# Later landing times in a planner, other homes for one branch's operands, and one branch product as four pairs of seven block products

## The chip, the cores and the metric

The kernel runs on one core of one Trainium2 chip. The metric is the device time of one execution in microseconds (us), the median of several runs, on the same chip for the kernels that are compared. TensorE multiplies matrices and writes to PSUM banks; VectorE and ScalarE do elementwise work and read the banks; GpSimd does some more; SyncE issues most of the transfers. Each engine works through its own queue in order.

## The reference

One layer of a decoder on 512 tokens of 1,024 channels, in fp32. A normed input is projected to everything that three branches need; each branch's output is gated and multiplied by its own square matrix, the three are summed under further gates, and a last product and a norm follow.

```python
h = rmsnorm(x, norm_g)
(aq, ak, av, ao, az, ai, af, bq, bk, bv, bz, bf, cu, cz, gates) = jnp.split(h @ w_in, SPLIT_POINTS, axis=-1)
hA = mlstm_chunkwise(conv and silu of aq, ak; av; ai, af)      # 4 heads of 256
yA = norm(hA) * ml_norm_g * sigmoid(ao) * silu(az)
yB = forgetting_attention(bq, bk, bv, bf) * silu(bz)           # 8 heads of 128
yC = multiscale_pool(cu, pool_w, pool_scale) * silu(cz)
yb = einsum('bsnw,nwd->bsnd', stack([yA, yB, yC], axis=2), w_branch)   # 3 x (512x1024 by 1024x1024)
merged = sum(sigmoid(gates) * yb, axis=2)
out = rmsnorm(x + merged @ w_out, final_g)
```

## The kernel before, in words

**Arithmetic.** Every fp32 operand is split into a high part (a cast to the type that TensorE multiplies, on ScalarE, `hi_of`, L288) and a low part (the rest, a subtraction on VectorE, `lo_of`, L291). A product is three matmuls, high by high, high by low and low by high (`mm3`, L300 to L302). Activations lie transposed, channels on the partitions and the 512 tokens along the row.

**Units and pairs.** A `unit` makes 128 output channels: 8 steps over the 1,024 input channels, 24 matmuls of 512 columns in one bank. A `pair` makes 256 output channels by a Strassen-Winograd scheme: the 2 by 2 block product takes seven block products (12 matmuls of 256 columns each, 84 in all) where two units take 48 matmuls of 512 columns. For it the activations come as seven operands (the blocks `A11`, `A12`, `A22` and the sums `s1` to `s4`, made once for all pairs of the same activations), and the weights as blocks and their sums, made for each pair. The weights of a pair come by two loads on SyncE's queue (L376, L380) and one that adds in flight on GpSimd's; VectorE adds two more sums (L294). A pair uses three of the four banks that projections have, named `x`, `yz` and `y4`; each holds more than one block product in turn, so between them ScalarE copies what is there into a side tile `e`. TensorE may not write the next block product into the bank before that copy is done:

```python
side(yz[:, H:], e[:, 2])                                    # ScalarE, L494
prod(x_[:, :H], 2, 0, sig["s2"], False, True, last=True)    # into x, on top
side(x_[:, :H], e[:, 1], -1.0)                              # ScalarE, L496
```

The block products of one pair follow each other in the banks `x`, `yz`, `yz`, `x`, `y4`, `yz`, `x`. In the trace a bank is named by what it makes and the pair's first number: `ak_ak_5x` is bank `x` of the pair that makes head 2's `ak`.

**What sets the order.** Nothing is ordered by hand. While the program is built, a planner (`Flow`) keeps a clock for each engine and a list of generators. Each of these says with `yield (engine, cost, earliest)` that its next instruction runs on that engine, for how long, and not before when; the planner always writes the instruction that can start first by its clocks. Tiles and banks are counted resources (`"w"` for 512-column work tiles, `"C"` and `"E"` for 1,024-column tiles, `"pj"` for the banks). So a number such as the `2.5` after a load, the time at which the load is taken to have landed, sets where the instruction that reads it stands in its engine's queue. Weights are prepared up to five items of TensorE's order ahead.

**The order of the work.** First the norm and head 0 of the mLSTM; heads 1 to 3 (`aq`, `ak`, `az`, `ao` as pairs, one plain gate unit each); four pool groups; eight attention heads in four rounds; the last gate pairs, `g_1_4` and `g_1_6`; then the branch products in the order mLSTM (`n = 0`), pool (`n = 2`), attention (`n = 1`), each as 8 units; then the output product. The results of the branches and the sigmoids of the gates go to DRAM (`y`, `g`) as they are made and come back later: `reload` loads a branch's output in eight pieces `yf` (L1625) and splits each into a home tile, and `load_gate` loads a gate tile `gt` (L1698). The evacuation of a unit multiplies the bank by the gate (L1716, L1718) and adds it to `merged`.

For each mLSTM head, `emat` loads a row `nmb` from DRAM and makes exponentials from it on ScalarE, four times the first of these two:

```python
nc.sync.dma_start(out=nmb, in_=rows[h:h + 1, :].partition_broadcast(P))       # L925
t = yield ("POOL", 0.9, t + 2.5)
nc.scalar.activation(out=es[:, P:], in_=nmb[:, s0 + P:], func=AF.Exp, bias=ac)  # L939
nc.scalar.activation(out=es[:, :P], in_=nmm[:, s0:s0 + P], func=AF.Exp, bias=ac)  # L941
```

The operands of the first branch have two homes of the kind `b` (1,024 columns), and the other two lie in tiles that the last attention head uses until then (`pmh`, `pml`, `vhi`, `emat`). The operands of the middle branch lie in the tiles of the normed input (`hT0`, `hT1`), free once the last gate product has read them.

## Time and profile before

| | |
|---|---|
| median of 3 runs | 863.16 us (862.78 to 864.06) |
| the profiled execution | 864.43 us, span 862.6 us |
| TensorE | 840.7 us busy, 97% of the span, 5882 matmuls in the record |
| VectorE | 638.9 us, 74% |
| ScalarE | 519.8 us, 60% |
| GpSimd | 110.2 us, 13% |
| mean granted clock of TensorE | 0.992 of full speed |
| transfers | 155.80 MB, 181 GB/s on average |

The span is the time from the first to the last instruction of the profiled execution; the time of that execution has some more around it, and the median is that of other executions. Busy shares are averages over stages that differ; where an engine waits is shown by the views of waits, of the chain of work and of the timeline.

### The profile page before, as it was taken

The numbers are of one execution on the slowest core, as the hardware profiler recorded it, in microseconds if no ns is written. First come the engines' busy times: TensorE is split into PE (matmuls) and PEld (weight loads), VectorE is DVE, ScalarE is ACT, GpSimd is POOL, SyncE is SP. The second block draws the span as 40 slices with busy tenths as digits, with TensorE's granted clock in tenths as the row PEclk, the third lists the DMA queues.
The fourth block names the chain that finished last, engine by engine and source line by source line (L and its number), as shares of the span: only waits on it lengthen the run. The fifth ranks groups of instructions, "written<-read, shape, count | busy, mean of one in ns | idle before, by whom it ended". The sixth has DMA issues, their size and how long they took to land.

```text
span 862.6 us, 14921 instructions
## 1 busy us (share of the span) xinstructions
PE 840.7 (97%) x5882; PEld 790.1 (92%) x5882; DVE 638.9 (74%) x1015; ACT 519.8 (60%) x881; POOL 110.2 (13%) x141
## 2 busy tenths in 40 slices
PE   8999999997999999999999999999999899999997
PEld 7888899997999999999999999999999778888886
DVE  4888987786988858888888787878877663445622
ACT  7569788747959748445567686567668532112323
POOL 0001521001110001011221222121210000000020
PEclk9999999998999999999999999999999999999999
DMA  9327865483684558487766876487873875564302
GB/s 342 104 75 224 223 163 155 140 255 89 171 244 102 149 152 234 148 219 204 195 209 172 248 198 177 112 250 199 233 180 116 305 267 192 171 244 132 106 32 98
DMA packets 60230, 155.80 MB, mean 181 GB/s; under 512 B 5364, under 2 KB 8820, under 8 KB 60160
## 3 DMA queue, kind: packets, MB, share of 16 engines
q1 hardware_dynamic: 45600, 125.91, 41.7%
q0 software_dynamic: 13840, 27.82, 19.9%
q10 hardware_dynamic: 720, 1.13, 0.4%
q8 instruction: 46, 0.75, 0.3%
q14 instruction: 24, 0.20, 0.1%
HBM read 140.13 MB, written 14.70 MB: 179 GB/s over the span
## 4 chain that ended last, share of the span: by engine, by line
PE 77%; DMA 10%; ACT 6%; DVE 5%; issue 1%; SPq 1%; POOL 0%; DVEq 0%; ACTq 0%; POOLq 0%
PE wb L302 4%; DMA R_None<-w_pairs 4%; PE wb L300 4%; PE wb L301 4%; DMA nmb<-rows 2%; PE out L302 2%; PE out L300 2%; PE out L301 2%; DVE lo L291 1%; DMA yf<-y 1%; ACT hi L288 1%; PE av L301 1%; PE av L302 1%; PE av L300 1%; DMA x<-x_in 1%
## 5 line engine op out<-in xcount | busy, mean ns | idle before, releaser
L291 DVE TENSOR_TENSOR lo<-R_None,hi 128x1024 fp32r<-128x1024 f32 (+1 forms) x168 | 180.8, 1087 | 31.7 <-ACT hi L288 31.0
L288 ACT CAST hi<-R_None 128x1024 fp32r<-128x1024 f32 (+1 forms) x168 | 153.6, 944 | 30.4 <-DVE R_None L294 17.2
L288 ACT CAST hi<-raw 128x1024 fp32r<-128x1024 f32 (+3 forms) x53 | 52.6, 1003 | 67.3 <-DMA raw<-w_units 59.4
L383 POOL DMA_DIRECT2D R_None<-w_pairs x42 | 51.1, 1217 | 328.4 <-DMA R_None<-w_pairs 172.3
L291 DVE TENSOR_TENSOR lo<-raw,hi 128x1024 fp32r<-128x1024 f32 (+3 forms) x53 | 61.1, 1161 | 14.4 <-ACT hi L288 14.1
L294 DVE TENSOR_TENSOR R_None<-R_None 128x512 f32<-128x512 f32 x84 | 58.1, 692 | 5.0 <-DMA R_None<-w_pairs 4.2
L1718 DVE TENSOR_TENSOR gt<-wb,gt 128x512 f32<-128x512 f32 x16 | 11.1, 691 | 37.2 <-PE wb L302 37.2
L1499 POOL TENSOR_SCALAR_AFFINE_SELECT nfb<-nfb 128x128 f32<-128x128 f32 x32 | 20.3, 643 | 73.9 <-DMA nfb<-rows 65.2
L291 DVE TENSOR_TENSOR lo<-R,hi 128x1024 fp32r<-128x1024 f32 (+1 forms) x24 | 25.7, 1083 | 3.3 <-ACT hi L288 3.3
L288 ACT CAST m<-mg 128x512 fp32r<-128x512 f32 x8 | 5.0, 621 | 35.8 <-DVE mg L294 35.8
L301 PE MATMUL out<-lo,m 128*128 128x512 f32 (+1 forms) x72 | 26.3, 366 | 0.0
L300 PE MATMUL out<-hi,m 128*128 128x512 f32 (+1 forms) x72 | 26.3, 366 | 0.0
L302 PE MATMUL out<-hi,m 128*128 128x512 f32 (+1 forms) x72 | 26.3, 366 | 0.0
L288 ACT CAST hi<-R 128x1024 fp32r<-128x1024 f32 (+1 forms) x24 | 21.9, 941 | 5.0 <-DVE R L294 3.2
L302 PE MATMUL wb<-yc,lo 128*128 128x512 f32 x64 | 24.9, 389 | 0.0
L300 PE MATMUL wb<-yc,hi 128*128 128x512 f32 x64 | 24.9, 389 | 0.0
L301 PE MATMUL wb<-yc,hi 128*128 128x512 f32 x64 | 24.9, 389 | 0.0
L1753 DVE TENSOR_TENSOR res<-out,res 128x512 f32<-128x512 f32 (+1 forms) x9 | 5.7, 632 | 17.9 <-PE out L302 17.8
L1756 ACT ACTIVATE fsq<-res 128x512 f32<-128x512 f32 (+1 forms) x9 | 5.3, 584 | 22.6 <-DVE res L1753 22.6
L1536 ACT ACTIVATE s<-s,mn 128x128 f32<-128x128 f32 (+3 forms) x32 | 17.7, 555 | 1.8 <-DVE mn L1525 1.7
L1525 DVE CUSTOM_DVE_ANT_0 s<-sB,nfb 128x128 f32<-128x128 f32 (+3 forms) x32 | 14.3, 486 | 5.4 <-issue 5.2
L960 DVE SCALAR_TENSOR_TENSOR cvaq<-aq,cs,cvaq 128x511 f32<-128x511 f32 (+2 forms) x18 | 13.4, 742 | 6.0 <-ACT cvaq L957 6.0
(2320 smaller groups left out, 3424.1 us busy)
## 6 DMA issues: line engine op xcount, KB each, us to landing
R_None<-w_pairs SPq DMA_DIRECT2D x42, 768.0 KB, 7.1
raw<-w_units SPq DMA_DIRECT2D x46, 512.0 KB, 4.3
R_None<-w_pairs SPq DMA_DIRECT2D x42, 512.0 KB, 5.2
R_None<-w_pairs POOLq DMA_DIRECT2D x42, 512.0 KB, 6.8
g<-g SPq DMA_DIRECT2D x12, 512.0 KB, 4.5
yf<-y SPq DMA_DIRECT2D x24, 256.0 KB, 5.6
gt<-g SPq DMA_DIRECT2D x24, 256.0 KB, 4.2
R<-w_pairs SPq DMA_DIRECT2D x6, 768.0 KB, 6.5
```

What stands on the lines that cost most here:

```text
L288: nc.scalar.copy(out=hi, in_=full)
L291: nc.vector.tensor_tensor(out=lo, in0=full, in1=hi.bitcast(F32), op=ALU.subtract)
L294: nc.vector.tensor_tensor(out=out_, in0=a, in1=c, op=ALU.add)
L300: nc.tensor.matmul(out_, lhsT=ah, rhs=bh, start=start, stop=False, **kw)
L301: nc.tensor.matmul(out_, lhsT=ah, rhs=bl, start=False, stop=False, **kw)
L302: nc.tensor.matmul(out_, lhsT=al, rhs=bh, start=False, stop=stop, **kw)
L383: nc.gpsimd.dma_start(out=r[:, 3 * Q:].rearrange("p (a c) -> p a c", a=2), in_=src[:, 3 * Q:].unsqueeze(1).to_broadcast([P, 2, Q]), accum_ ...
L960: nc.vector.scalar_tensor_tensor(out=acc[:, j:], in0=srcs[c][:, :S - j], scalar=col(C_CONV, ci * 4 + 3 - j), in1=acc[:, j:], op0=ALU.mult, ...
L1499: nc.gpsimd.affine_select(out=nf[i][:, i * P:], in_=nf[i][:, i * P:], pattern=[[-1, P]], compare_op=ALU.is_ge, fill=NEG, base=0, channel_m ...
L1525: nc.vector.tensor_tensor_reduce(out=ss[i][:, :n], in0=os_[i][:, :n], in1=nf[i], scale=-P ** -0.5, scalar=-NEG, op0=ALU.add, op1=ALU.min, ...
L1536: nc.scalar.activation(out=s_, in_=s_, func=AF.Exp, bias=ms[i][0], scale=-1.0, accum_out=sme)
L1718: nc.vector.tensor_tensor(out=g_, in0=o, in1=g_, op=ALU.mult)
```

## The change

1. **Landing times.** The planner's times from the issue of a load to its reader go up: `rows` 2.5 to 4.5, `nmb` 2.5 to 6.8, `nfb` (attention) 4.0 to 8.0, `yf` 2.5 to 6.0, `gt` 2.5 to 4.6, and those of the stores of `y` and `g`.
2. **Homes.** The operands of the first branch go to `b` tiles, all but one low part; the second half of `merged` goes to the tiles that held them. Loads of `yf` may be issued as soon as the first home is free; the reload of the third branch is queued after the first branch's units.
3. **The middle branch.** Its product is made by four pairs. A new function, `sides_c`, makes the seven operands from eight loads `ycf`; a pair's result is merged by two multiplies of 512 columns and one sum of 1,024.

```diff
@@ -82,7 +82,10 @@
     for n in (0, 2, 1):
-        u += [("U", "wb", n, d) for d in range(KT)]
+        if n == 2:
+            u += [("P", ("wb", n, 2 * i), ("wb", n, 2 * i + 1)) for i in range(KT // 2)]
+        else:
+            u += [("U", "wb", n, d) for d in range(KT)]
...
@@ -923,7 +926,7 @@
             nc.sync.dma_start(out=nmb, in_=rows[h:h + 1, :].partition_broadcast(P))
-            t = yield ("POOL", 0.9, t + 2.5)
+            t = yield ("POOL", 0.9, t + 6.8)
...
@@ -1618,12 +1621,13 @@
                 ty = yield ("wait", ("y", n, i))
-                th = yield ("wait", ("home", n, i))
+                yield ("wait", ("home", n, 0))
                 tw = yield ("get", "w", 1)
                 t = yield ("SP", 0.06, max(tw, ty))
                 f_ = work(f"yf{n}{i}{c}")
                 nc.sync.dma_start(out=f_, in_=yd[n, i][:, c])
-                t = yield ("ACT", a_cost(S), max(t + 2.5, th))
+                th = yield ("wait", ("home", n, i))
+                t = yield ("ACT", a_cost(S), max(t + 6.0, th))
...
@@ -1639,34 +1643,85 @@
-            return (tg("pmh"), tg("pml")) if i == 2 else (tg("vhi"), tg("emat"))
+        def home(nm):
+            def at(i):
+                if i == 3:
+                    lo = st.tile([P, 2, S], F32R, tag="emat", name=f"{nm}3l", bufs=1)
+                    return b(f"{nm}3h", (P, 2, S), F32R), lo
+                return [b(f"{nm}{i}{x_}", (P, 2, S), F32R) for x_ in ("h", "l")]
+            return at
...
+        def sides_c():
+
+            big = [st.tile([P, 4, 4, H], F32R, tag=f"hT{i}", name=f"yc{i}", bufs=1) for i in range(2)]
+            t = yield ("get", "E", 2)
+            f_ = [b(f"ycf{q}", (P, 4, H)) for q in range(4)]
+            tq = []
+            for q in (2, 3, 0, 1):
+                for i in range(2):
+                    ty = yield ("wait", ("y", 2, 2 * (q % 2) + i))
+                    t = yield ("SP", 0.06, max(t, ty))
+                    nc.sync.dma_start(out=f_[q][:, 2 * i:2 * i + 2],
+                                      in_=yd[2, 2 * (q % 2) + i][:, :, (q // 2) * H:(q // 2 + 1) * H])
+                tq.append(t + 9.0)
+            done = {}
+
+            def parts(name, q, home, t):
+                t = yield ("ACT", a_cost(D), t)
+                hi, lo = home if home else [b(f"yc{name}{x_}", (P, 4, H), F32R) for x_ in ("h", "l")]
+                hi_of(hi, f_[q])
+                t = yield ("DVE", v_cost(D), t)
+                lo_of(lo, f_[q], hi)
+                sig_c[name] = (hi, lo)
+                done[name] = t
+
+            def total(o, a_, c_, op, t):
+                t = yield ("DVE", v_cost(D), t)
+                nc.vector.tensor_tensor(out=f_[o], in0=f_[a_], in1=f_[c_], op=op)
+                done["f", o] = t
...
+            t = max(tq)
+            yield from parts("A22", 3, home(0), t)
+            yield from parts("A11", 0, home(1), t)
+            yield from total(3, 2, 3, ALU.subtract, done["A22"])
+            yield from parts("A12", 1, home(2), t)
+            yield from total(2, 0, 2, ALU.subtract, done["f", 3])
+            yield from parts("s1", 3, home(3), done["f", 3])
+            yield from total(0, 3, 0, ALU.subtract, done["f", 3])
+            yield from total(1, 1, 0, ALU.add, max(done["f", 0], done["A12"]))
+            yield from parts("s2", 0, None, done["f", 0])
+            yield from parts("s4", 1, None, done["f", 1])
+            yield from parts("s3", 2, None, done["f", 2])
...
@@ -1680,11 +1735,10 @@
         fl.add(free_a(), 1)
-        reload(0, home_a, 1)
+        reload(0, home("ya"), 1)
         while gates_left:
             filler()
-        fl.put("w", 2)
-        homes_left()
+        fl.add(sides_c(), 1)
...
@@ -1696,7 +1750,7 @@
                 nc.sync.dma_start(out=g_, in_=gd[n, d // 2][:, d % 2])
-                fl.done["gt", n, d] = t + 2.5
+                fl.done["gt", n, d] = t + 4.6
...
         branch(0, True, False)
-        for name, k in (("qk", 2), ("v", 1)):
-            fl.put(name, k)
-        branch(2, False, False)
+        for i in range(4):
+            fl.done["home", 1, i] = fl.t["PE"]
+        reload(1, home("yb"), 2)
+        fl.need(("ys", 2))
+        for i in range(KT // 2):
+            cell = [None]
+
+            def merge(cell, i, t):
+                c_ = cell[0]
+                for c in range(2):
+                    tg = yield ("wait", ("gt", 2, 2 * i + c))
+                    t = yield ("DVE", v_cost(S), max(t, tg))
+                    nc.vector.tensor_tensor(out=c_[:, c], in0=c_[:, c], in1=gate.pop((2, 2 * i + c)),
+                                            op=ALU.mult)
+                    fl.put("w", 1, t)
+                t = yield ("DVE", v_cost(D), t)
+                add(merged[i], merged[i], c_)
+                fl.put("C", 1, t)
+
+            for c in range(2):
+                load_gate(2, 2 * i + c)
+            pair(("wb", 2, 2 * i), ("wb", 2, 2 * i + 1), two(cell, f"ybc{i}"),
+                 lambda t, cell=cell, i=i: fl.add(merge(cell, i, t), 1), sig_c)
```

Over the whole program TensorE has 5994 instructions instead of 5850, VectorE 1044 instead of 1017, ScalarE 852 instead of 827, GpSimd 150 instead of 146, SyncE as many as before. Below stand instructions as they follow each other in an engine's queue, before the change and after it; the lines of the changed kernel have other numbers (L288 is L291, L494 and L496 are L497 and L499, L939 is L942).

**The third head.** ScalarE's queue before the change, at head 2's `ak` pair (`ak_4_ak_5`: its bank copies are those of `x`, `yz`, `x`, `y4`):

```order
L494 COPY ak_4_ak_5e_2085<-ak_4_ak_5yz_2087 128x256
L288 CAST pAl1_2023<-e1_1424 128x128
L957 ACTIVATE cvaq21_2146<-aq2_2047,cs_71 128x512
L939 ACT_TABLE_LOAD
L939 ACTIVATE e2_2143<-nmb2_2137,aT_203 128x384
L496 ACTIVATE ak_4_ak_5e_2085<-ak_4_ak_5x_2068 128x256
L494 COPY ak_4_ak_5e_2085<-ak_4_ak_5y4_2150 128x256
L941 ACTIVATE e2_2143<-nmm2_2139,aT_203 128x128
```

After the change, at the same pair:

```order
L497 COPY ak_4_ak_5e_2088<-ak_4_ak_5yz_2090 128x256
L499 ACTIVATE ak_4_ak_5e_2088<-ak_4_ak_5x_2071 128x256
L960 ACTIVATE cvaq21_2167<-aq2_2048,cs_71 128x512
L291 CAST hi23_2_2169<-R23_None_1812 128x1024
L497 COPY ak_4_ak_5e_2088<-ak_4_ak_5y4_2145 128x256
L291 CAST hi23_1_2198<-R23_None_1812 128x512
L1065 ACTIVATE dn1_2234<-num10_2138 128x1
L1065 ACTIVATE dn1_2234<-num11_2158 128x1
L1065 ACTIVATE dn1_2234<-num12_2187 128x1
L291 CAST hi24_0_2240<-R24_None_1988 128x1024
L942 ACTIVATE e2_2206<-nmb2_2122,aT_203 128x384
```

The copies of `yz`, `x` and `y4` stood around the exponential of `nmb2`, two of them behind it; they now all stand ahead of it, and the casts of the next weights (`hi23`, `hi24`) stand between.

**The last gate pair.** ScalarE's queue before the change, at the pair `g_1_6_g_1_7`, with the splits of the first branch's operands (`ya2`, `ya3`, from the loads `yf02` and `yf03`):

```order
L494 COPY g_1_6_g_1_7e_8258<-g_1_6_g_1_7yz_8260 128x256
L288 CAST ya3vhi_8333<-yf030_8326 128x512
L288 CAST ya3vhi_8333<-yf031_8328 128x512
L288 CAST hi65_8338<-raw65_8273 128x1024
L288 CAST ya2pmh_8343<-yf020_8322 128x512
L496 ACTIVATE g_1_6_g_1_7e_8258<-g_1_6_g_1_7x_8240 128x256
L288 CAST ya2pmh_8343<-yf021_8324 128x512
L494 COPY g_1_6_g_1_7e_8258<-g_1_6_g_1_7y4_8347 128x256
```

After the change, from the end of the gate pair before it (`g_1_4_g_1_5`):

```order
L497 COPY g_1_4_g_1_5e_8105<-g_1_4_g_1_5y4_8163 128x256
L1539 ACTIVATE s73_8027,sm73_8191<-s73_8027,mn73_8055 128x512
L291 CAST ya2h_8202<-yf020_8099 128x512
L291 CAST hi63_2_8223<-R63_None_7808 128x1024
L291 CAST ya2h_8202<-yf021_8121 128x512
L291 CAST ya3h_8253<-yf030_8125 128x512
L291 CAST ya3h_8253<-yf031_8141 128x512
L291 CAST pB7h_8227<-tpB70_8247 128x512
L497 COPY g_1_6_g_1_7e_8267<-g_1_6_g_1_7x_8233 128x256
L291 CAST hi63_3_8285<-R63_None_7808 128x1024
```

The splits of `ya2` and `ya3` stood between the copies of the last gate pair; they now stand behind the last copy of the pair before it and ahead of the first copy of the last one.

**The first of the middle branch's pairs.** ScalarE's queue after the change, at the pair `wb_2_0_wb_2_1`, which was two units without copies before (`yb` are the third branch's operands, `hi73` the next pair's weights):

```order
L291 CAST hi73_0_8728<-R73_None_8619 128x1024
L497 COPY wb_2_0_wb_2_1e_8763<-wb_2_0_wb_2_1x_8748 128x256
L291 CAST yb0h_8779<-yf100_8732 128x512
L291 CAST hi73_2_8794<-R73_None_8619 128x1024
L291 CAST yb0h_8779<-yf101_8734 128x512
L497 COPY wb_2_0_wb_2_1e_8763<-wb_2_0_wb_2_1yz_8765 128x256
L291 CAST yb1h_8815<-yf110_8736 128x512
L291 CAST yb1h_8815<-yf111_8738 128x512
L499 ACTIVATE wb_2_0_wb_2_1e_8763<-wb_2_0_wb_2_1x_8748 128x256
```

The casts of the loads `yf10` stand between the copies of `x` and `yz`. Those loads stand in SyncE's queue behind the weights of the last pair (`R75`):

```order
L379 DMA R75_None_8713<-w_pairs 128x2x512
L383 DMA R75_None_8713<-w_pairs 128x1536
L1628 DMA yf100_8732<-y10_208 128x512
L1628 DMA yf101_8734<-y10_208 128x512
L1628 DMA yf110_8736<-y11_209 128x512
L1628 DMA yf111_8738<-y11_209 128x512
```

Before the change the same loads stood among the loads of the gate and output weights, ahead of the first branch's gates:

```order
L1625 DMA yf100_8419<-y10_208 128x512
L1625 DMA yf101_8421<-y10_208 128x512
L1625 DMA yf110_8443<-y11_209 128x512
L1625 DMA yf111_8453<-y11_209 128x512
```

## Rows read from the trace of the kernel before

**Rows 1.** What TensorE waited for: total us, times, longest.

```profile
PE ak_ak_5x L300 <- ACT ak_ak_5e L496: 5.3, 1, 5.3
PE g_g_7x L300 <- ACT g_g_7e L496: 2.2, 1, 2.2
PE ak_ak_3yz L300 <- ACT ak_ak_3e L494: 1.8, 1, 1.8
...
PE bz_bz_5yz L302 <- DVE lo L291: 0.5, 1, 0.5
```

**Rows 2.** The chain of work from 182 to 200: start, us, what.

```profile
183.17 1.13 DVE lo L291
184.30 0.60 DVE aq L294
...
187.32 9.02 DMA nmb<-rows
...
196.41 1.28 ACT L939
...
198.64 0.58 PE ak_ak_5x L300
```

**Rows 3.** ScalarE's timeline at the first head: start, us, instruction, idle before it.

```profile
107.00 0.62 ACT L939 ACTIVATE e<-nmb,aT 128x384 f32<-128x384 f32 x1 [3.90 <-DMA nmb<-rows]
...
108.92 0.35 ACT L494 COPY ak_ak_3e<-ak_ak_3yz 128x256 f32<-128x256 f32 x1
```

**Rows 4.** ScalarE's timeline at the last gate product.

```profile
673.71 1.20 ACT L288 CAST ya3vhi<-yf 128x512 fp32r<-128x512 f32 x2 [4.85 <-DMA yf<-y]
...
676.28 0.37 ACT L496 ACTIVATE g_g_7e<-g_g_7x 128x256 f32<-128x256 f32 x1
```

**Rows 5.** TensorE's timeline, the 22nd matmul after 198.64.

```profile
203.30 0.32 PE L300 MATMUL az_az_5x<-hT,hi 128*128 128x256 f32 x1
```

**Rows 6.** TensorE's timeline in a block product without a wait.

```profile
91.36 0.28 PE L300 MATMUL aq_aq_3x<-s2h,hi 128*128 128x256 f32 x1
...
92.80 0.28 PE L300 MATMUL aq_aq_3y<-hT,hi 128*128 128x256 f32 x1
```

**Rows 7.** Busy time by stretch; PEclk, after POOL, is the granted clock.

```profile
198.60:203.30 4.70, 4.66 (x21) 4.66 (x22) 3.62 (x6) 4.70 (x11) 0.00 (x0) 0.50 0.77 113
109.20:113.00 3.80, 3.67 (x25) 3.43 (x26) 1.45 (x3) 3.80 (x11) 1.23 (x1) 1.00 0.59 146
```

**Rows 8.** TensorE's timeline at the last gate product and the first matmul of each branch.

```profile
676.71 0.39 PE L300 MATMUL g_g_7x<-s3h,hi 128*128 128x256 f32 x1 [2.17 <-ACT g_g_7e L496]
...
678.54 0.63 PE L300 MATMUL wb<-ya0h,hi 128*128 128x512 f32 x1
...
725.77 0.39 PE L300 MATMUL wb<-yc,hi 128*128 128x512 f32 x1
...
769.29 0.39 PE L300 MATMUL wb<-yb0h,hi 128*128 128x512 f32 x1
```

**Rows 9.** VectorE's timeline at the first gated multiply.

```profile
695.61 0.69 DVE L1716 TENSOR_TENSOR mg<-wb,gt 128x512 f32<-128x512 f32 x1 [6.66 <-DMA gt<-g]
```

**Rows 10.** ScalarE's timeline around 182, one instruction behind the other.

```profile
181.48 1.04 ACT L288 CAST hi<-R_None 128x1024 fp32r<-128x1024 f32 x1
182.42 0.37 ACT L494 COPY aq_aq_5e<-aq_aq_5y 128x256 f32<-128x256 f32 x1
182.68 0.63 ACT L288 CAST hi<-R_None 128x512 fp32r<-128x512 f32 x1
183.20 0.63 ACT L288 CAST pA1h<-e 128x512 fp32r<-128x512 f32 x1
```

**Rows 11.** SyncE's queue from 629, and its loads: KB each, us to landing.

```profile
629.94 0.55 SPq L376 DMA_DIRECT2D R_None<-w_pairs  x1
...
631.23 2.86 SPq L1625 DMA_DIRECT2D yf<-y  x4
...
yf<-y SPq DMA_DIRECT2D x4, 256.0 KB, 8.1
```

More of the change, by code (lines that the diff above doesn't have):

```diff
@@ L468, in trunk, with pair @@
         sig = {}
-        def pair(a, c, into, after):
+        def pair(a, c, into, after, sig=sig):
             i = item("P", a, c)
@@ L886, in gates @@
             nc.gpsimd.dma_start(out=rows[0:4], in_=nm)
-            fl.done["rows"] = t + 2.5
+            fl.done["rows"] = t + 4.5
             mt = b4
@@ L1336, in gen @@
                 nc.sync.dma_start(out=dst, in_=tl)
[L1337 to L1338 removed]
+                fl.put("C", 1, t_ + 4.5)
+                fl.done[key] = t_ + 6.0
             fl.add(gen(), 0)
@@ L1652, in free_a @@
             fl.done["home", 0, 0] = fl.done["home", 0, 1] = t
-            yield ("wait", ("oB", BH - 1))
-            t = yield ("get", "pm", 1)
+            t = yield ("get", "C", 2)
             fl.done["home", 0, 2] = t
-            t = yield ("get", "v", 1)
+            t = yield ("get", "C", 1)
             t = yield ("get", "em", 1)
             fl.done["home", 0, 3] = t
-        def homes_left():
-            t = fl.t["PE"]
-            fl.put("S", 8)
-            fl.grab("S", 8)
-            big = [st.tile([P, KT, S], F32R, tag=f"hT{i}", name=f"yc{i}", bufs=1) for i in range(2)]
-            for n in (1, 2):
-                for i in range(4):
-                    fl.done["home", n, i] = t
-            reload(2, lambda i: [t_[:, 2 * i:2 * i + 2] for t_ in big], 1)
-            reload(1, lambda i: [b(f"yb{i}{x_}", (P, 2, S), F32R) for x_ in ("h", "l")], 2)
+            yield ("wait", ("oB", BH - 1))
@@ new lines, in free_a, with merged_tile, home @@
+            yield ("get", "pm", 1)
+            yield ("get", "v", 1)
+            fl.done["merged"] = 0.0
+        def merged_tile(i):
+            if i < 2:
+                return c_tile(f"mg{i}")
+            while "merged" not in fl.done:
+                fl.push()
+            return st.tile([P, 2, S], F32, tag=("pmh", "vhi")[i - 2], name=f"mg{i}", bufs=1)
+        sig_c = {}
+        def sides_c():
[23 more added lines that the diff above has]
+                done["f", o] = t
+            def home(n):
+                return [t_[:, n] for t_ in big]
+            t = max(tq)
[10 more added lines that the diff above has]
+            yield from parts("s3", 2, None, done["f", 2])
+            t = done["s3"]
+            fl.put("E", 2, t)
+            fl.put("C", 2, t)
+            fl.done["ys", 2] = t
@@ L1730, in trunk @@
         branch(0, True, False)
-        for name, k in (("qk", 2), ("v", 1)):
-            fl.put(name, k)
-        branch(2, False, False)
+        for i in range(4):
[19 more added lines that the diff above has]
+                 lambda t, cell=cell, i=i: fl.add(merge(cell, i, t), 1), sig_c)
+        fl.put("w", 2)
+        while fl.chains and len(fl.free["C"]) < 1:
+            fl.push()
         mh, ml_ = [st.tile([P, KT, S], F32R, tag=f"hT{i}", name=f"m{i}", bufs=1) for i in range(2)]
```

17 lines of the change are left out of this document (6 added, 11 removed).

## The prediction, made before the changed kernel ran

> **What bounds the kernel now.** I read the page first: TensorE is busy for nearly the whole span, so an edit counts only where TensorE waits, runs at the low clock, or has fewer columns to stream. The second view was therefore the list of what TensorE waited for. Between its start and the last gate product there are few entries, and three of them name a copy on ScalarE that empties a PSUM bank: 5.3, 2.2 and 1.8 us [rows 1]. The third view, the chain of work, says why that copy was late. For the longest, a load of `nmb` was issued at 187.32 and landed 9.02 us later; ScalarE stood before the exponential that reads it, loaded its function table for 1.28, ran the exponential, and only then made the copy, which released TensorE at 198.64 [rows 2]. The copy's operand had been there all along; it was queued behind an instruction that waited for a transfer. The same picture stands at 107: the exponential of the first head sat 3.90 us for its `nmb`, with the copy for `ak_ak_3yz` behind it [rows 3]. At 673.71 it is a load of `yf`: 4.85 us of idle ScalarE before `ya3vhi`, and the copy for the last gate product starts at 676.28 [rows 4].
>
> The fourth view is TensorE's timeline after such a wait. From 198.64 to 203.30 stand 22 matmuls [rows 2, 5], which at the pace of 12 in 1.44 us (91.36 to 92.80, 0.120 each) [rows 6] would be 2.64; they took 4.66. In between the granted clock was 1.2 GHz instead of 2.4, half [rows 7]. So that wait cost 5.3 + 2.0 = 7.3. The 12 matmuls from 676.71 to 678.54 took 1.83 instead of 1.44 [rows 8]: 2.2 + 0.4 = 2.6. The wait of 1.8 brought no drop of the clock, 1.00 behind it [rows 7].
>
> The last stretch to read is that of the branch products. The first branch runs from 678.54 to 725.77, 47.23 us, the middle one from 725.77 to 769.29, 43.52 us [rows 8], though both are 8 units of 24 equal matmuls. The 3.7 us between them are the rest of the low clock, two waits for a weight's low part, and a slightly slower pace on the borrowed operand tiles. The two waits come from VectorE, which stood 6.66 us before its first gated multiply because the gate `gt` was loaded late [rows 9].
>
> **The change, part by part.** *Landing times.* They are numbers in the planner's clock; no instruction is added by them, only places move. At the first head the copy of `ak_ak_3yz` now stands in front of the exponential; nothing that TensorE needs within the next product follows it: -1.8. At the third head (the first place shown above) all four copies of the `ak` product stand in front of it. The next copy behind it is that of the `az` product. I bound that one: SyncE issues the pair's loads once the third last pair is split, and `nmb` after them. Counting VectorE's queue at its rates (1.13 for 1,024 columns, 0.60 for 512 [rows 2]) the issue falls about 1 us later than before against TensorE's work, so with the same 9.02 the exponential runs 1 us later too. TensorE by then is one product and a half further on in its own order, and ScalarE's list from there to the `az` copy is about 3.2 us (two splits at 0.94, the rest short [rows 10]). The copy comes some 1.4 us before the product that needs the bank, so I take the full -7.3; the other end is that the 1.4 are gone and up to 5.3 comes back.
>
> *Other homes.* The operands of the first branch no longer wait for the last attention head's tiles, and their splits stand ahead of the last gate product's copies; the loads are issued one and a half gate products earlier. The copies behind them have about 2 us to spare when `yf` lands after 5.7 to 8.1 us: -2.6. The gate `gt` is now issued before the 2 MB of the middle branch instead of after them, so the multiply no longer holds VectorE for long, and the operands all lie in tiles of one kind: the first branch falls to the middle one's 43.52, -3.7. Against this, its gate loads now share the queue with those 2 MB; a gate that is 2 to 3 us late only delays the multiply, and the fourth bank gives TensorE three units of cover.
>
> *The middle branch in pairs.* Removed: 192 matmuls of 512 columns, 43.52 us [rows 8]. Added: 4 x 7 x 12 = 336 of 256 columns at 0.120: 40.3. That is -3.2. The price of the 256-column matmul is from hundreds of equal ones in this trace [rows 6], so its bounds are narrow (0.117 to 0.122: -4.2 to -2.5). The Trainium skill states it otherwise: its page "TensorE: Matmul & The Clock Gate", section "Back-to-back issue gap", gives sustained figures of about 81 ns at 128 columns and 131 at 512. An estimate between these two is 98 ns at 256, by which a pair would take 8.2 us instead of 6.3 and the four pairs would lose 7.7 us. The trace disagrees at both widths, and the measurement decides.
>
> The operands of the pairs need 7 casts on ScalarE and, on VectorE, 7 subtractions and 4 sums of 1,024 columns. They stand in the first branch's stretch. VectorE there has 18 instructions of 1.13 and 11 of 0.60, 26.9 us in 43.5, so they are hidden, with 16 us to spare. In the pairs' own stretch VectorE has 8.8 us a pair, 4.8 for the third branch's operands and 3.4 for its first weights, less 5.2 done earlier: 38.2 of 40.3. That is close, but it is ahead of TensorE.
>
> *A new wait.* Call U the end of the first branch's products. In ScalarE's queue `yb0h`, which reads a load `yf`, now stands before the copy of the first pair's `yz` bank, and TensorE needs that copy for its sixth block product, at U + 5 x 1.44 = U + 7.2. SyncE issues that load behind the last pair's weights, which wait for the split of the first pair's last part, which in VectorE's queue follows the multiply of unit 6, free at U - 5.44 (43.52 / 8): -5.44 + 0.60 + 1.13 = U - 3.7. The nearest row is a `yf` right behind a pair's loads: it was issued 1.29 us after the first of these two and landed after 8.1 [rows 11]. So U - 2.4 for the issue, U + 5.7 for the landing; then 0.52, 0.94, 0.52 and 0.26 on ScalarE [rows 10]: U + 7.9. TensorE waits 0.7, with handovers 0.8. With a load as slow as the 9.02 of `nmb` it is 1.7, with one of 7.3 or less it is 0.
>
> *Small waits.* The order of some 460 us changes in detail. Before, the longest wait in the stretch from the third head to the last gate pairs is 0.5 [rows 1]; I add one such, between 0 and a wait of the copy's kind (the second rival).
>
> **Sum.** -1.8 - 7.3 - 2.6 - 3.7 - 3.2 + 0.8 + 0.5 = -17.3. The profiled execution took 864.43 (span 862.6 and 1.8 around it), so 847.1; it lies 1.3 above the median of the runs, 863.16, so I predict **845.8**.
>
> **The rivals.**
> 1. *The first pair waits longer.* The load behind the last pair's weights, or VectorE at 38 of 40 us, costs 2 to 3 us, and the clock falls as after the 2.2 us wait, adding up to 2: 848 to 851. For it speaks that there is no slack at that copy; against it that only a load slower than all of these makes it so.
> 2. *A wait of the old kind elsewhere.* The 1.4 us at the `az` copy are used up, or another head's exponential, or a `yf`, holds ScalarE. Up to 7.3 with the clock: 849 to 853. For it speaks that before had three such; against it that each such load is now issued further ahead of its reader, and that the copies behind each have cover.
> 3. *The 256-column matmul costs more than half of the wide one.* Where it took 0.1295 (48 x 0.2267 / 84) the pairs would gain nothing, and the time would be 849. The rows of 0.120 stand against it. That is the case to which the skill's figures belong.
> 4. *The new landing times move no wait.* Only the pairs gain: 860. The order shows the copies moved, so I keep little for it.
> 5. *Slower.* VectorE works in order, and the operand chain stands between multiplies that wait for gates. If these came so late that the first pair's last part is not split when TensorE wants it, TensorE stands at U + 5.8. The part is due at U - 3.7, so 9.5 us of lateness are free, and another 17.3 are needed before the kernel is slower: 27 us, four times the 6.66 that one gate cost. Price then: 864 and up.
>
> **How the numbers follow.** Chances: forecast 0.64 (843 to 848.3), rival 1 0.10, rival 2 0.16, rival 3 0.02, rival 4 0.02, rival 5 0.03, something better or in between 0.03. The low end: without the 0.8 and the 0.5, and with 0.117 a matmul, 843.5, so 843. The high end is one whole wait of 7.3 on top: 853. A difference under 0.2% (1.7 us) can't be told from none. Faster by more: all but rivals 4 (half of it) and 5, 0.95; the same 0.02; slower 0.03.
>
> **What would show it.** Right: TensorE's list of waits has no entry for `ak_ak_5x`, `ak_ak_3yz` or the last gate product over 1 us; the clock stays at 2.4 GHz around 200 and 680; the first branch takes 43.5 us, the four pairs 40.3 to 42; one wait of 0 to 1.7 us at the first pair's `yz`, with `yb0h` and `yf` ahead of it in the chain. Wrong: a wait on a copy behind `nmb` at the third head, a late `gt` that holds VectorE until a bank is missing, pairs that take over 42, or a new entry over 2 us between 200 and 660.

## The result, and the profile after

The changed kernel takes 853.19 us (median, 852.84 to 855.6) against 863.21 for the kernel before: a ratio of 0.9884 with a 95% interval of 0.9867 to 0.9901, so 10 us faster (8.5 to 11.5). The forecast was 17.3 less. Its profiled execution took 853.38, with a span of 851.4 and a mean clock of 0.997. One execution below, of the kernel with the landing time of `nmb` put back, ran at a mean clock of 0.848 and took 900.26 us; neither its time nor its trace is used.

The list of what TensorE waited for, after (total us, times, longest); it answers to [rows 1]:

```profile
PE wb_wb_1yz L303 <- ACT wb_wb_1e L497: 2.3, 1, 2.3
PE vbv_bv_1z L303 <- ACT hi L291: 1.7, 1, 1.7
PE aq_aq_3y L305 <- DVE lo L294: 1.3, 1, 1.3
PE vbv_bv_1z L304 <- DVE lo L294: 1.1, 2, 0.9
```

The three entries of 5.3, 2.2 and 1.8 us are gone; none of the copies of those pairs is in the list. Two places are new: the first of the middle branch's pairs (`wb_wb_1yz`), and the turned pair that makes the attention's `bv` (`vbv_bv_1z`), of which the prediction says nothing. (In a turned pair activations and weights change roles in the matmul; it makes `bv` for two attention rounds.)

TensorE's timeline after, at the third head's `ak` product and its gate product, at the two ends of the part around the turned pair, and at the first matmul of each branch and of the output product (start us, us, instruction); it answers to [rows 8]:

```profile
193.03 0.28 PE L303 MATMUL ak_ak_5x<-s3h,hi 128*128 128x256 f32 x1
...
217.45 0.28 PE L303 MATMUL g_g_7yz<-hT,hi 128*128 128x256 f32 x1
...
395.73 0.28 PE L303 MATMUL bq_bk_0yz<-hT,hi 128*128 128x256 f32 x1
...
469.93 0.36 PE L303 MATMUL bq_bk_2x<-hT,hi 128*128 128x256 f32 x1
...
670.60 0.40 PE L303 MATMUL wb<-ya0h,hi 128*128 128x512 f32 x1
...
714.70 0.28 PE L303 MATMUL wb_wb_1x<-yc,hi 128*128 128x256 f32 x1
...
757.41 0.40 PE L303 MATMUL wb<-yb0h,hi 128*128 128x512 f32 x1
...
801.51 0.40 PE L303 MATMUL out<-hi,m 128*128 128x512 f32 x1
```

The same matmuls before, where [rows 8] does not show them:

```profile
227.06 0.28 PE L300 MATMUL g_g_7yz<-hT,hi 128*128 128x256 f32 x1
...
404.38 0.28 PE L300 MATMUL bq_bk_0yz<-hT,hi 128*128 128x256 f32 x1
...
473.55 0.28 PE L300 MATMUL bq_bk_2x<-hT,hi 128*128 128x256 f32 x1
...
812.81 0.39 PE L300 MATMUL out<-hi,m 128*128 128x512 f32 x1
```

The granted clock by stretch, after (the clock is the number behind the five busy times), at the third head and at the turned pair; it answers to [rows 7]:

```profile
193.00:200.00 7.00, 7.00 (x61) 7.00 (x60) 5.11 (x9) 5.49 (x13) 0.11 (x1) 1.00 0.41 68
424.50:432.00 7.50, 6.11 (x35) 5.62 (x36) 7.24 (x9) 3.63 (x5) 0.00 (x0) 0.77 0.01 3
```

At the third head the clock now stays at its upper level, 2.4 GHz; it falls to 1.2 GHz at the turned pair instead, behind TensorE's wait there (0.50 from 426.3 to 429.5; the 0.77 is a mean over both levels).

The starts of the same matmuls in the two traces give where the time went. All stretches hold the same work but the middle branch.

| stretch | before | after | moved | forecast |
|---|---|---|---|---|
| start to the gate product of the third head (227.06, 217.45) | 227.06 | 217.45 | -9.6 | -9.1 |
| from there to the first branch | 451.48 | 453.15 | +1.7 | -2.1 |
| first branch | 47.23 | 44.10 | -3.1 | -3.7 |
| middle branch | 43.52 | 42.71 | -0.8 | -2.4 |
| third branch | 43.52 | 44.10 | +0.6 | 0 |
| output product to the end | 49.82 | 49.85 | 0.0 | 0 |
| span | 862.6 | 851.4 | -11.2 | -17.3 |

In the second stretch the part around the turned pair, from the pair `bq_bk_0_1` bank `yz` to the first product of the next round (`bq_bk_2`), took 69.17 before and 74.20 after: +5.0. The last gate product gives some -2.5 (its wait of 2.2 is gone, and its last 12 matmuls take 1.51 us instead of 1.83), so -0.8 is left for everything else there.

**The turned pair.** SyncE's queue after, from 409, then ScalarE's timeline, then the second load with its KB and the us to landing:

```profile
409.53 0.55 SPq L379 DMA_DIRECT2D R_None<-w_pairs  x1
410.12 2.87 SPq L1497 DMA_DIRECT2D nfb<-rows  x4
413.03 0.43 SPq L383 DMA_DIRECT2D R_None<-w_pairs  x1
```

```profile
423.14 0.62 ACT L291 CAST hi<-R_None 128x512 fp32r<-128x512 f32 x1 [8.90 <-DMA R_None<-w_pairs]
423.67 1.04 ACT L291 CAST hi<-R 128x1024 fp32r<-128x1024 f32 x1
```

```profile
R_None<-w_pairs SPq DMA_DIRECT2D x1, 768.0 KB, 10.1
```

A pair's weights come in two loads on SyncE's queue. Here the four loads `nfb` of the first attention head (640 KB, each row sent to all partitions) stand between the two. The second part lands at 423.1. ScalarE stands 8.90 us before its cast, though that cast is for the pair `bz` behind (R46, the weights with this number), which TensorE begins at 445.1; the cast behind it, `hi<-R`, is the one that the turned pair needs. It is the picture of [rows 2] once more, with a weight where `nmb` was. Of the 5.0 us, 2.8 are the two waits at `vbv_bv_1z` (1.7 and 1.1); most of the rest is the clock, for behind them the matmuls start 0.21 us apart instead of 0.12 until 428.4.

**The first middle pair.** ScalarE's timeline after, and SyncE's queue with the last pair's weights and the loads `yf`:

```profile
721.60 0.62 ACT L291 CAST yb0h<-yf 128x512 fp32r<-128x512 f32 x1 [4.85 <-DMA yf<-y]
722.12 1.04 ACT L291 CAST hi<-R_None 128x1024 fp32r<-128x1024 f32 x1
723.41 0.62 ACT L291 CAST yb0h<-yf 128x512 fp32r<-128x512 f32 x1 [0.25 <-DMA yf<-y]
723.94 0.37 ACT L497 COPY wb_wb_1e<-wb_wb_1yz 128x256 f32<-128x256 f32 x1
```

```profile
713.93 0.55 SPq L379 DMA_DIRECT2D R_None<-w_pairs  x1
714.53 0.59 SPq L383 DMA_DIRECT2D R_None<-w_pairs  x1
715.17 3.90 SPq L1628 DMA_DIRECT2D yf<-y  x7
```

The wait is the one that was forecast, with the queue that was forecast. U, the end of the first branch, is 714.70. The weights' load was put at U - 3.7 and stands at U - 0.8; the copy was to end at U + 7.9 and does at U + 9.6. The `yf` load itself was quicker than the 8.1 us taken for it: its cast runs 6.4 us behind its issue.

Why so late? Busy times of the engines in three parts of the first branch (PE, PEld, DVE, ACT, POOL), then ScalarE's wait at the end of the first part and SyncE's queue ahead of it:

```profile
670.60:686.45 15.85, 15.85 (x72) 12.98 (x71) 3.69 (x7) 3.16 (x3) 0.00 (x0) 1.00 1.03 363
686.45:709.11 22.66, 22.66 (x100) 18.54 (x99) 22.54 (x23) 11.91 (x13) 2.41 (x2) 1.00 0.88 283
709.11:714.70 5.59, 5.59 (x27) 4.54 (x26) 3.66 (x5) 2.54 (x3) 1.22 (x1) 1.00 1.10 237
```

```profile
685.36 1.05 ACT L291 CAST hi<-raw 128x1024 fp32r<-128x1024 f32 x1 [8.94 <-DMA raw<-w_units]
```

```profile
672.10 5.38 SPq L1687 DMA_DIRECT2D ycf<-y  x8
...
678.16 0.43 SPq L343 DMA_DIRECT2D raw<-w_units  x1
```

VectorE works 29.9 of the first branch's 44.1 us, close to the 26.9 of 43.5 of the prediction. But it works 3.7 of the first 15.9 us and 22.5 of the next 22.7. It starts behind a weight that was issued behind the eight loads `ycf`, and then its whole list comes in one piece, with the split that frees the last pair's weights at its end.

### The profile page after: what moved, and what is told of

It reads as the page before. It is cut to its first block, busy times and chain, and to the rows that moved or that the text cites. A ratio compares the mean times of both kernels' runs of the same rounds, so it can differ in the third digit from the quotient of the medians.

```text
span 851.4 us, 15247 instructions
## 1 busy us (share of the span) xinstructions
PE 835.8 (98%) x6026; PEld 792.1 (93%) x6026; DVE 663.1 (78%) x1042; ACT 535.4 (63%) x906; POOL 114.0 (13%) x145
## 4 chain that ended last, share of the span: by engine, by line
PE 45%; DVE 2%; issue 1%; DMA 1%; ACT 1%; SPq 0%; DVEq 0%; ACTq 0%
PE wb L304 2%; PE wb L303 2%; PE wb L305 2%; PE out L304 2%; PE out L305 2%; PE out L303 2%; PE tpB L1562 1%; DMA yf<-y 1%; DVE lo L294 1%; DVE ycf L1703 1%; PE sB L304 0%; PE sB L303 0%; PE oB L303 0%; PE oB L304 0%; PE oB L305 0%
## 5 line engine op out<-in xcount | busy, mean ns | idle before, releaser
L294 DVE TENSOR_TENSOR lo<-R_None,hi 128x1024 fp32r<-128x1024 f32 (+1 forms) x184 | 197.8, 1091 | 30.2 <-ACT hi L291 29.7
L291 ACT CAST hi<-R_None 128x1024 fp32r<-128x1024 f32 (+1 forms) x184 | 169.1, 945 | 45.4 <-DVE R_None L297 26.0
L386 POOL DMA_DIRECT2D R_None<-w_pairs x46 | 56.0, 1217 | 461.4 <-DMA R_None<-w_pairs 211.5
L294 DVE TENSOR_TENSOR lo<-raw,hi 128x1024 fp32r<-128x1024 f32 (+3 forms) x45 | 51.5, 1151 | 25.7 <-ACT hi L291 25.4
L291 ACT CAST hi<-raw 128x1024 fp32r<-128x1024 f32 (+3 forms) x45 | 44.2, 994 | 40.9 <-DMA raw<-w_units 34.6
L297 DVE TENSOR_TENSOR R_None<-R_None 128x512 f32<-128x512 f32 x92 | 63.3, 689 | 2.5 <-DMA R_None<-w_pairs 1.7
L291 ACT CAST hi<-R 128x1024 fp32r<-128x1024 f32 (+1 forms) x24 | 22.0, 942 | 8.7 <-DVE R L297 7.2
L291 ACT CAST m<-mg 128x512 fp32r<-128x512 f32 x8 | 5.0, 620 | 23.5 <-DVE mg L297 23.4
L303 PEld LDWEIGHTS out<-hi,m 128*128 128x128 f32 x72 | 13.6, 189 | 2.3
L304 PEld LDWEIGHTS out<-lo,m 128*128 128x128 f32 x72 | 13.6, 189 | 2.2
L305 PEld LDWEIGHTS out<-hi,m 128*128 128x128 f32 x72 | 13.6, 189 | 2.2
L386 POOL DMA_DIRECT2D R<-w_pairs x6 | 7.2, 1206 | 51.8 <-DMA R<-w_pairs 18.8
L1857 POOL TENSOR_TENSOR res<-res,fgb 128x512 f32<-128x512 f32 x4 | 5.2, 1296 | 65.3 <-ACT fsq L1833 65.1
```

Of the source, the lines that this page charges most:

```text
L291: nc.scalar.copy(out=hi, in_=full)
L294: nc.vector.tensor_tensor(out=lo, in0=full, in1=hi.bitcast(F32), op=ALU.subtract)
L297: nc.vector.tensor_tensor(out=out_, in0=a, in1=c, op=ALU.add)
L303: nc.tensor.matmul(out_, lhsT=ah, rhs=bh, start=start, stop=False, **kw)
L304: nc.tensor.matmul(out_, lhsT=ah, rhs=bl, start=False, stop=False, **kw)
L305: nc.tensor.matmul(out_, lhsT=al, rhs=bh, start=False, stop=stop, **kw)
```

## The experiments

Where a kernel has a ratio, it is to the kernel before, timed on the same chip in turn; a time "at 863.2" is that ratio times the 863.2 of the kernel before. Two ratios whose intervals overlap are not told apart.

**One load moved.** R46's second load goes ahead of the four `nfb`; no other instruction moves. (R46 belongs to the pair `bz` of the first round; the expectation names another.)

```diff
-                tn = yield ("SP", 0.2, tn)
+                tn = yield ("SP", 0.2, max(tn, t + 0) if h == 0 else tn)
```

> The changed kernel with one instruction moved: on SyncE's queue the second load of the weights of the pair bq, bk of head 3 (R46) goes ahead of the four loads nfb of the first attention head instead of behind them. Nothing else changes place on any engine. Theory A (the four loads between the two parts make the second part late, ScalarE stands 8.9 us before its cast, and the casts for the turned pair bv stand behind it): the waits of 1.7 and 1.1 us at vbv_bv_1z go, the clock stays at 2.4 GHz there, and the stretch loses the 4.8 us that it is behind the pace: 848.4, between 847.5 and 849.5. Rival B (the part is slow because the transfers as a whole are busy there, not because of its place): the cast still waits most of its 8.9 us, TensorE's wait moves or stays: 851 to 853.

Measured: 0.9831 (0.9809 to 0.9853), 4.6 us less than the changed kernel at 863.2. `vbv_bv_1z` is not in the list of waits, and the stretch of 74.20 us takes 69.28 (396.06 to 465.34). ScalarE's timeline and the load of that part in this kernel:

```profile
416.43 0.62 ACT L291 CAST hi<-R_None 128x512 fp32r<-128x512 f32 x1 [1.85 <-DMA R_None<-w_pairs]
416.95 1.04 ACT L291 CAST hi<-R 128x1024 fp32r<-128x1024 f32 x1
```

```profile
R_None<-w_pairs SPq DMA_DIRECT2D x1, 768.0 KB, 6.0
```

The part is issued 2.6 us earlier (at 410.45 instead of 413.03) and lands in 6.0 us instead of 10.1. Its place behind the `nfb` cost it both. Theory A holds.

What the place costs depends on the clock too. In the seven traces that have this load behind the `nfb`, the stretch took 72.81 to 75.47 us, 3.6 to 6.3 more than before: 72.81 where the clock stayed at its upper level (1.00 from 420 to 432), up to 75.47 where it was low for longest (0.59 from 424.5 to 432, where the changed kernel has 0.77).

**The casts of the third branch's loads put behind the first pair's copies.**

```diff
-                t = yield ("ACT", a_cost(S), max(t + 6.0, th))
+                t = yield ("ACT", a_cost(S), max(t + (6.0, 12.0, 6.0)[n], th))
```

> The changed kernel with the planner's landing time of the third branch's loads yf at 12 us instead of 6. The order of TensorE, GpSimd and SyncE stays, on ScalarE the casts yb go behind the four copies of the first middle pair, and VectorE's subtractions follow. Theory A (the copy of the first pair's yz waits only behind the casts of yf): the wait of 2.3 us at wb_wb_1yz goes, and nothing takes its place, 850.8 (850 to 851.5). Rival B (VectorE is so late by then that the second pair's weights or the evacuations are the next to be missing): a wait of 1 to 2 us at the second pair or at the third branch's first matmul, 852 to 853.5.

Measured: 0.9847 (0.9831 to 0.9863). `wb_wb_1yz` is gone from the list and the four pairs take 41.69 us instead of 42.71. Not nothing: 1.1 us of wait are new at the fourth pair (`wb_wb_7y`, 0.8 for a low part and 0.3 for its high part), where ScalarE's cast of a weight of the third branch stands ahead of the pair's own. Between A and B, nearer to A. The time alone would say more than the edit did: it is 3.2 us less than the changed kernel's, but 1.0 of that is the pairs'; 1.4 more come from the turned pair's stretch, which the edit does not touch (72.81 us here).

**The landing times alone, on the kernel before.** The seven numbers, and nothing else.

> The kernel before with all seven landing times of the change, the old homes and no pairs in the middle branch. Up to the last gate pairs its order is that of the changed kernel. Theory A (the landing times move the copies ahead of the exponentials, and also put nfb between R46's two loads): at the start of the pool groups it is 8 to 9 us ahead of before, after the turned pair bv 5 ahead; the last gate product no longer waits (2.6 more), but the operands of the first branch and the first gate stay late, so the first branch keeps its 47 us: about 855.5 (854 to 858). Rival B (the gain at the third head comes from something else in the change): within 2 us of before.

Measured: 0.9881 (0.9866 to 0.9895), 852.9 at 863.2, no different from the whole change and faster than both theories said. Its trace reaches the first branch at 669.29 (changed kernel 670.60, before 678.54), has the waits at `vbv_bv_1z` (1.3 and 1.1), and none at the heads or the last gate product. The first branch takes 46.22 us, the other two 43.52. So the landing times bring the gain of the heads and of the gate product, 1.0 of the 3.1 us at the first branch, and the loss at the turned pair. In the traces the three branches together take 133.3 us here and 130.9 in the changed kernel, 2.4 less by homes and pairs; in the times, with their intervals, that can't be seen.

**The middle branch as units again, landing times and homes kept.**

> The changed kernel with the middle branch as eight plain units from the tiles of the normed input, loaded and split as before the change; landing times and homes stay. Up to the last gate pair the order is that of the changed kernel. Theory A (the pairs save 3.2 us of matmuls and give back 2.4 in the first pair's wait): 0.8 us above the changed kernel, 854.0 (853 to 855.5). Rival B (the operand chain of the pairs also delays the first branch's gates and weights): the time is at or below that of the changed kernel, 851.5 to 853.

Measured: 0.9871 (0.9855 to 0.9888), 852.1 at 863.2, which the intervals do not tell from the changed kernel; as a time it lies in the range of B. In the trace the first branch takes 44.10, the middle one 43.56 and the third 44.07. The pairs cost the first branch nothing, so the mechanism of B is not there. They bring 0.85 of 43.56 us in the changed kernel's profiled execution, and that is luck: in the four other traces with the same wait at the first pair (2.0, 2.8, 2.9 and 4.4 us instead of 2.3) they took 43.91, 45.92, 44.84 and 47.39 us, no less than units, because the clock fell behind the wait as well. Here is the clock behind the wait in the changed kernel, then in the one with the wait of 2.0 us (the next experiment):

```profile
726.00:728.00 2.00, 2.00 (x19) 2.00 (x18) 2.00 (x4) 2.00 (x5) 0.00 (x0) 1.00 1.10 264
```

```profile
726.00:728.00 2.00, 2.00 (x11) 2.00 (x11) 2.00 (x3) 2.00 (x4) 0.00 (x0) 0.50 1.08 255
```

So with that wait the pairs save nothing that can be counted on; what they save without it, the experiments below show.

**The third branch's last low part in another tile.**

```diff
-                    lo = st.tile([P, 2, S], F32R, tag="emat", name=f"{nm}3l", bufs=1)
+                    lo = st.tile([P, 2, S], F32R, tag="emat" if nm == "ya" else "pml", name=f"{nm}3l", bufs=1)
```

> The changed kernel with the low part of the third branch's last operand (yb3l) in the tile pml instead of emat; no instruction changes its place. Theory A (operands streamed from emat make the products of the third branch slow: 44.1 us in the changed kernel, 43.5 in the kernel before, which had it in a tile of kind b): the third branch takes 43.5, 0.6 less in all. Rival B (the slower pace comes from what else runs beside it, the output weights' loads or the merge): it stays at 44.1.

Measured, from the trace of a single execution: the third branch takes 44.10 us. The tile `pml` is no better; the expectation failed.

**Three edits together**: the load moved, the casts put behind, `pml`.

> The changed kernel with three edits: R46's second load ahead of nfb, the casts yb behind the first middle pair's copies, and yb3l in pml. If the three causes are apart from each other (A): the turned pair bv loses its 4.8 us, the four pairs take 41.7 instead of 42.7, the third branch 43.5 instead of 44.1: 853.2 - 6.4 = 846.8 (846 to 848), a ratio of 0.981. If VectorE's lateness is the one cause behind the middle pairs (B), the pairs keep 43 us or more and the time is 848.5 to 850.

Measured: 0.9796 (0.9775 to 0.9817), 845.6 at 863.2. The turned pair's stretch takes 69.14, the pairs 41.64, the third branch 44.09. The first two edits add up, so their causes are apart; the third does nothing.

**The landing time of `nmb` alone put back.** In this order `nfb` stands behind both of R46's loads.

```diff
-            t = yield ("POOL", 0.9, t + 6.8)
+            t = yield ("POOL", 0.9, t + 2.5)
```

> The changed kernel with the landing time of nmb alone back at 2.5 us. In this order the copies of the third head's pair stand again behind the exponential, and nfb no longer splits the loads of R46. Theory A (this one number brings both the 9 us gain at the heads and the 4.8 us loss at the turned pair): the waits on ak_ak_5x of about 5 and on ak_ak_3yz of about 2 are back, with 2 us at the low clock, the waits at vbv_bv_1z are gone: 853.2 + 9.1 - 4.8 = 857.5 (856 to 859). Rival B (the loss at the turned pair comes from another landing time or from the homes): the waits at vbv_bv_1z stay, 861 to 863.

Measured: 0.995 (0.993 to 0.9969), 858.9 at 863.2. The same kernel once more, with its trace:

> The changed kernel with the landing time of nmb alone back at 2.5 us, once more for its trace. Theory A (this one number brings both the gain at the heads and the loss at the turned pair): TensorE's list of waits has ak_ak_5x with about 5 us and ak_ak_3yz with about 2, the clock falls to 1.2 GHz behind the first, and no entry for vbv_bv_1z. Rival B (the loss comes from another landing time or the homes): vbv_bv_1z is in the list with more than 1 us.

Its list of waits and the clock around 200:

```profile
PE ak_ak_5x L303 <- ACT ak_ak_5e L499: 5.3, 1, 5.3
PE wb_wb_1yz L303 <- ACT wb_wb_1e L497: 2.8, 1, 2.8
PE ak_ak_3yz L303 <- ACT ak_ak_3e L497: 1.8, 1, 1.8
```

```profile
197.00:202.00 5.00, 2.83 (x13) 2.84 (x14) 1.79 (x3) 4.99 (x10) 1.85 (x2) 0.63 0.37 51
202.00:206.00 4.00, 4.00 (x24) 4.00 (x24) 4.00 (x8) 3.97 (x7) 0.00 (x0) 0.61 0.38 70
```

Both waits at the heads are back to the tenth, with the low clock, and TensorE reaches the third head's gate product at 228.07 (before 227.06, changed kernel 217.45); `vbv_bv_1z` is gone, and its stretch takes 69.14 us. One number makes both: the heads' 9 us, and, by where the first attention head's loads then fall in SyncE's queue, the turned pair's 5.

**The eight loads `ycf` issued by GpSimd.**

```diff
-                    nc.sync.dma_start(out=f_[q][:, 2 * i:2 * i + 2],
+                    nc.gpsimd.dma_start(out=f_[q][:, 2 * i:2 * i + 2],
```

> The changed kernel with the eight loads ycf issued by GpSimd instead of SyncE; no other instruction moves. Theory A (the eight loads hold SyncE's queue for 5.4 us, the weights of a unit behind them come late, ScalarE stands 8.9 us before their cast, VectorE's whole list for the middle branch's operands starts late, and so the last pair's weights and the loads yf behind them): that cast waits 4 to 5 us less, the loads yf are issued 1 to 3 us earlier against TensorE's work, and the wait of 2.3 us at the first pair's yz shrinks to 0 to 1: 851.2 to 852. Rival B (the weights are late because the same bytes are in flight, whoever issues them): the cast waits as long, the time is that of the changed kernel, 853.

Measured: 0.9843 (0.9823 to 0.9863), 849.6 at 863.2, below what A said, and the four pairs take 40.73 us, 2.0 less than the changed kernel's; the first pair's `yz` is not in the list. ScalarE's waits for the unit weights, then the first pair (the first branch ends at 715.01), then SyncE's load of the last weights:

```profile
680.73 1.05 ACT L291 CAST hi<-raw 128x1024 fp32r<-128x1024 f32 x1 [6.87 <-DMA raw<-w_units]
683.93 1.06 ACT L291 CAST hi<-raw 128x1024 fp32r<-128x1024 f32 x1 [2.15 <-DMA raw<-w_units]
...
719.75 0.62 ACT L291 CAST yb0h<-yf 128x512 fp32r<-128x512 f32 x1 [2.74 <-DMA yf<-y]
...
721.74 0.37 ACT L497 COPY wb_wb_1e<-wb_wb_1yz 128x256 f32<-128x256 f32 x1
```

```profile
712.47 0.55 SPq L379 DMA_DIRECT2D R_None<-w_pairs  x1
```

The weight's cast stands 13.0 us behind the first branch's start instead of 14.8, the last weights are issued at U - 2.5 instead of U - 0.8, the copy stands at U + 6.7 instead of U + 9.2. The mechanism is A's. Its size is less than expected at the weight (1.7 us, not 4 to 5), and there B has a part: the cast of the weight ahead of it, the first of the two, comes 5.0 us later than in the changed kernel (9.8 instead of 4.8 behind the branch's start), because its load, issued at 670.82, lands 9.8 us later with the `ycf` in flight, where it took 4.8 in the changed kernel. The 1.7 was enough.

**Four edits together**: the load moved, the casts behind, `ycf` by GpSimd, and `yb3l` in a tile of kind `b`.

> The changed kernel with four edits: R46's second load ahead of nfb, the casts yb behind the first middle pair's copies, the eight loads ycf issued by GpSimd, and yb3l in a tile of kind b. If the causes are apart from each other (A): the turned pair bv loses 4.9 us, the four pairs take 40.5 (40.3 to 41) instead of 42.7, the third branch 43.5 instead of 44.1: 853.2 - 4.9 - 2.2 - 0.6 = 845.5, a ratio of 0.979 or a little less. If they share a cause (B), the pairs keep 41.6 and the time is 846.5. For the third branch alone: theory A (a tile of kind b streams at the full pace, emat and pml don't): 43.5; rival B (the pace there has another cause): 44.1.

Measured: 0.9793 (0.9778 to 0.9808), 845.3 at 863.2, the fastest of all but not told apart from the three edits. The span is 844.1. The list of waits has nothing above 1 us behind the first microseconds; the longest entry there and the one in the pairs, and TensorE's timeline:

```profile
PE aq_aq_3y L305 <- DVE lo L294: 0.8, 1, 0.8
...
PE wb_wb_7y L305 <- DVE lo L294: 0.4, 1, 0.4
```

```profile
709.54 0.28 PE L303 MATMUL wb_wb_1x<-yc,hi 128*128 128x256 f32 x1
...
750.32 0.40 PE L303 MATMUL wb<-yb0h,hi 128*128 128x512 f32 x1
...
793.86 0.39 PE L303 MATMUL out<-hi,m 128*128 128x512 f32 x1
```

The pairs take 40.78 us, the third branch 43.54. So a tile of kind `b` does give the 43.5 of the kernel before.

**The low parts 32 bytes further into `emat`.**

> The changed kernel with the low parts ya3l and yb3l still in the tile emat, but starting 8 elements (32 bytes) further into it; no instruction changes its place. Theory A (the pace hangs on where in memory an operand starts: emat and pml start at another multiple of 32 bytes than all tiles of kind b): the first and the third branch take 43.5 us each instead of 44.1, 1.1 less in all, 852.1. Rival B (the pace hangs on the tile, or on what else runs): both stay at 44.1.

Measured: 0.9875 (0.9853 to 0.9897). The first branch takes 43.90, the third 43.89: a third of the 0.57 us above 43.5 is gone, and neither theory fits; where the tiles start in memory is in no trace. Its wait at the first pair was 4.4 us, with the changed kernel's order.

## Why the prediction was off

**The time.** 845.8 was forecast, with a range up to 853.0; 853.19 was measured. The sign and the main mechanism were right, the size too large. Between the spans of the profiled executions 6.1 us are missing: 3.8 from the second stretch of the table, 1.6 from the middle branch, 0.6 and 0.6 from the first and third branch, less 0.5 that the heads gave above the forecast. Another 1.1 come from the sum's last step: it took 1.3 off, by which the profiled execution before lay above its median; after the change that distance is 0.2.

**Landing times, the heads and the gate product: right.** Forecast -1.8 and -7.3, measured -9.6 together. The 1.4 us of cover at the `az` copy were not put to the test, and that was luck: `nmb` landed 5.7 us behind its issue there, not the 9.02 that the sum took. The last gate product no longer waits, as forecast. That the copy was late and not its operand is shown by the kernel with `nmb` put back, where 5.3, 1.8 and the low clock return by one number.

**"Small waits", +0.5: the step that failed.** It priced 460 us of changed order by the longest wait that stood there before. What came was a wait of the copy's kind, at another place and with another load: 5.0 us at the turned pair. It is the second rival, which had 0.16 and named exponentials and `yf` as the holders; the holder was a weight. The change of places was in the order of SyncE's queue, open to be read: four loads between the two halves of one pair's weights. The prediction goes through what stands behind the loads that were given new landing times. It does not ask what those loads now stand in front of. The expectation's 4.8 us and the measured 4.9 (74.20 to 69.28) agree, and the cause is shown by moving that one load. The prediction's sign for this, a new entry over 2 us between 200 and 660, did not come: the entries are 1.7 and 1.1, and most of what is left of the 5.0 is the clock.

**The new wait, +0.8: right in its place, too small.** It was 2.4 us (the copy ended at U + 9.6, and TensorE needed it at U + 7.2). This is the first rival, which had 0.10 and named the load behind the last pair's weights, 2 to 3 us, and a fall of the clock; the clock fell in the four other traces and not in this one. The sum took the last weights' load at U - 3.7, because VectorE was to be free then: "26.9 us in 43.5, so they are hidden, with 16 us to spare". Of 14.2 idle us 12.2 lay ahead of the work. Moving the loads that held its start took the wait away. In the five traces that have this order at the first pair, and `ycf` on SyncE, the wait was 2.0, 2.3, 2.8, 2.9 and 4.4, always above the 0.7 of the prediction.

**Other homes, -3.7: -3.1.** The low clock and the two waits went, as forecast; 1.0 of the 3.1 is the landing times' (46.22 us with them alone). "The operands all lie in tiles of one kind" was wrong: one low part stays in `emat`. In the third branch, where it was forecast at nothing, that costs 0.57 us, as 43.54 with a tile of kind `b` shows; that the same 0.57 of the first branch has the same cause is not shown by itself.

**The pairs, -3.2: right but for the wait.** With the wait taken out, the changed kernel's pairs take 42.71 - 2.4 = 40.3, and 40.73 and 40.78 in the two kernels with `ycf` on GpSimd's queue, 2.8 and 2.7 less than units. By the Trainium skill's page "TensorE: Matmul & The Clock Gate", section "Back-to-back issue gap", the four pairs would have lost 7.7 us against units (an estimate, worked out in the prediction). The trace disagrees: 40.73 us for 336 matmuls is 0.121 each.

**The range.** Its upper end was one whole wait of the old kind. Two losses came at once, of 5.0 and 2.4, each above the term that stood for it; the measured 853.19 lies 0.2 above that end.

## What to carry to other kernels

A number that moves one load in a planner's clock moves the loads behind it too. Read in the new order of the queue that issues transfers which two parts of one operand were separated, and who waits in order for the later part: here four loads between the two loads of one pair's weights gave back 5.0 of the 12.1 us that the landing times won at the heads and the gate product. A busy share over a stretch is no cover: ask when the engine can start, and what stands at the end of its list. Price a wait of TensorE with and without a fall of the clock behind it; one execution doesn't tell which it will be. Issue the loads of one operand side by side, and let a cast of something that is needed late stand behind the copies that are needed now.

## What the runs showed that was not expected

A load of 768 KB landed in 6.0 us ahead of four small loads that go to all partitions, and in 10.1 behind them, counted from its own issue; over all traces 5.9 to 7.2 ahead of them and 8.9 to 10.3 behind them.

A wait of the same place and much the same length has a low clock behind it in one execution and not in another. At the first middle pair the clock stayed at its upper level behind 2.3 us and fell to the lower behind 2.0; at `ak_ak_3yz` it was 1.00 behind 1.8 us before [rows 7], and in the kernel with `nmb` put back it fell behind the same 1.8 (0.57 from 109 to 113). What decides it is open.

The place of a moving operand has a small price that no queue explains: a branch of 192 matmuls takes 43.52 to 43.56 us with all operands in tiles of kind `b` or `hT`, and 44.07 to 44.10 with one low part in `emat` or `pml`, in every trace. Shifted by 32 bytes within `emat` it was 43.9. Why is open.
